# A transformer block on one core: far attention scores from packed copies, softmax statistics on another queue, transposes twelve slots behind

## The chip, the core and the metric

The kernel runs on one core of one Trainium2 chip. The metric is the device time of one execution in microseconds, less being better; the time before is the median of three runs. All arithmetic is fp32 in effect: a matmul operand is split into a high and a low part in the fp32r format, and a product is two or three matmuls.

## The reference

One block over 1024 tokens of 1024 channels: a gated causal convolution branch, a dilated window attention with 16 heads of 64, a gated sum of both, then a feed-forward layer with a short convolution. The attention, which the change is about, is this (cut):

```python
DILATION_GROUPS = ((128, 1), (512, 4), (2048, 16))
for window, dilation in DILATION_GROUPS:
    o_g, lse_g = dilated_window_attention(q, k, v, slopes, window, dilation)
    ...
mix = jax.nn.softmax(jnp.stack(lses), axis=0)
o = jnp.einsum('gbsh,gbshd->bshd', mix, jnp.stack(outs))
...
# in dilated_window_attention: a query sees keys that lie a multiple of `dilation` back, up to `window`
scores = scores - slopes[:, None, None] * dist
scores = jnp.where(valid[None, :, None], scores, -jnp.inf)
m = jnp.max(scores, axis=-1, keepdims=True)
p = jnp.exp(scores - m)
```

The three groups together are one softmax in which a key counts once for each group that it is in, so the kernel adds the logarithm of that count to the score, as part of a mask that holds the slope as well.

## The kernel before

The kernel projects q, k, v (with norms) and parks them in DRAM; then comes the attention loop; then the output projections and the feed-forward layer.

**Units of a head.** The 1024 queries are eight tiles of 128, numbered 0 to 7. Half 0 is tiles 0 to 3; each needs keys of tiles up to its own. Half 1 is tiles 4 to 7 and has two parts. Its *near* part takes the keys of tiles 4 to 7 (for tile 4 also tile 3). Its *far* part takes the keys 0 to 511 that are left; they lie more than 128 tokens back, where only every fourth distance counts, so queries 512 to 1023 and keys 0 to 511 fall into four residues modulo 4, and within a residue 128 queries meet 128 keys. `scored` makes each score with two matmuls (line 916 with the high part of the keys, 917 with the low part), each 128x128 for the far part; before the change their operands are views of q, kh, kl with a step of four elements (`fourth_of`).

**Slots.** The loop runs over `slots`: eight a head, one score unit each. `SCORES` gives them: half 0 has (3), (2), (1), (0); half 1 has far, (7), (6), (4, 5). Before, a head begins with half 1 (places 0 to 3) and then does half 0 (places 4 to 7); only the last head has them the other way. What happens in a slot:

- `score`: matmuls into PSUM, and on VectorE (DVE) `least` (line 920), which adds the mask, takes the maximum and copies to SBUF as tile `pf` (far) or `p`;
- `fill`: steps of a filler, the gate and convolution output products, three matmuls of 128x512 each (names `gate`, `ya`). `FRONT` and `BEHIND` say how many at which of eight places; `START` adds some to the first slots, `TAIL` holds for the slots after the last score. There are 192 steps;
- `flip`: BACK slots after the scores, TensorE transposes the powers into `pp` or `pp_far` (line 1007); ScalarE and DVE split them into `ph`, `pl` (`split`);
- `weigh`: one slot later, the products with v (lines 1044, 1045, output `o`); `result`: ScalarE copies to `ot`, two DMAs write it (`do`);
- `powers`: exp on ScalarE, with the sums, in tile `own` for half 1.

**Normalizing before the transposes.** Half 0's powers are divided by their sums one slot later: `share`, a reciprocal on DVE and a scaling on GpSimd (`times`, line 962). Half 1's queries have two parts in two layouts (near: 128 consecutive tokens on the partitions; far: one residue), so each part needs the other's maximum and sum in its own layout. `give` writes `own` to DRAM (`dst`, 4 KB, the far layout right after the far powers, the near layout after unit (4, 5)); `take` reads `dst` in the other layout into `other`; `combine` makes the factors `both` on DVE and ScalarE, and eight `times` scale the powers on GpSimd, the far ones first. Before, `give` is issued on ScalarE's queue (line 978) and `take` on SyncE's (line 982), and `combine` stands six slots after the far scores.

**Queues.** In this stretch ScalarE, DVE and TensorE keep the written order. SyncE, which issues all loads and most stores and is called the load queue here, and GpSimd are ordered by the build's scheduler. Each engine works its instructions in order: a `take` that waits for its `give` to land holds up what stands behind it on the load queue. `head(h + 1)` loads q, kh, kl (two halves of the partitions each) and the mask m at place 1, `values(h)` loads v (tokens) and vf (residues) at place 0. The tiles q, kh, kl, m, v, vf, own, other, p and pf are double.

Of the kernel before, what the change touches and what calls it, by code (L numbers as in the profile page):

```python
# [14 lines left out]
F32R = mybir.dt.float32r  # L15
# [6 lines left out]
P = 128  # L22
# [3 lines left out]
H = 16  # L26
# [6 lines left out]

LAG = 2
WARM = 7
FRONT = (1, 1, 1, 0, 0, 0, 1, 1)
BEHIND = (1, 0, 1, 1, 1, 0, 1, 0)
BACK = 8
START = (2, 1, 1, 1, 0, 0, 0, 0)
TAIL = (2, 1)  # L40
PLAIN = (10, 11)
LATE = (12, 13, 14, 15)
PAIRS = ((0, 1), (2, 3), (4, 5), (6, 7), (8, 9))
# [15 lines left out]
def block_kernel(ctx: ExitStack, tc: tile.TileContext, x, xT, x0, g2, pack, mask,  # L59
                 w_first, w_ch, w_qkv, w_co, w_ao, w_o, w_up, w_down, out):  # L60
    nc = tc.nc
    act, dve, pool, pe, sp = nc.scalar, nc.vector, nc.gpsimd, nc.tensor, nc.sync
# [7 lines left out]
    def big_ps(name):  # L70
        return psA.tile([P, T], F32, tag="A", name=name)
# [232 lines left out]
    if True:  # L304
# [331 lines left out]
        for ch in range(6):  # L636
            kind, g8 = ch % 3, ch // 3
            wpieces = [wpiece(w_qkv[kind * 2 + g8, :, 2 * j : 2 * j + 2, :], f"qkv{ch}_{j}") for j in range(4)]
            for tt in range(8):
# [3 lines left out]
                if len(tails) > LAG:  # L643
                    t = tails.pop(0)
# [112 lines left out]
        tiles = {}  # L757
# [137 lines left out]
    p2b = p2b_cm.__enter__()  # L895
    if True:
# [4 lines left out]
        def ready2(tag, shape, dt, bufs, name):  # L901
            return laid.pop(tag) if tag in laid else p2b.tile(shape, dt, tag=tag, bufs=bufs, name=name)
# [9 lines left out]
        fourth_of = lambda t, r: t.rearrange("p (j r) -> p r j", r=4)[:, r]  # L912
        by_fourth = lambda t: t.rearrange("p (i a r) -> p i r a", r=4, a=32)

        def scored(s, qs, kh, kl):
            pe.matmul(s, qs, kh, start=True, stop=False)
            pe.matmul(s, qs, kl, start=False, stop=True)  # L917

        def least(pt, s, m, nm):
            dve.tensor_tensor_reduce(out=pt, in0=s, in1=m, scale=-1.0, scalar=3e38,  # L920
                                     op0=ALU.add, op1=ALU.min, accum_out=nm)
# [3 lines left out]
        def score(h, tiles, units):  # L925
            q, kh, kl, m = tiles
            made = []
            if not score_banks:
                pair = big_ps(f"s_{h}_{units[0]}")
                score_banks.extend((pair[:, 512:], pair[:, :512]))  # L930
            s = score_banks.pop()
            tag, size = ("pf", 512) if units == ("far",) else ("p" + "".join(map(str, units)),
                                                            sum((i + 1 - lowest(i)) * P for i in units))
            whole = ready2(tag, [P, size], F32, 2, f"{tag}_{h}")
            if units == ("far",):
                for r in range(4):
                    scored(s[:, r * P : (r + 1) * P], fourth_of(q[:, 512:], r),
                           *(fourth_of(t[:, 0:512], r) for t in (kh, kl)))
                for r in range(4):
                    pt = whole[:, r * P : (r + 1) * P]  # L940
                    pts[h, "far", r] = pt, own[h][:, 1, r]
                    least(pt, s[:, r * P : (r + 1) * P], m[:, 512:640], own[h][:, 1, r, 0:1])
                    made.append(pts[h, "far", r])
                return made
            at = 0
            for i in units:
                ks = slice(lowest(i) * P, (i + 1) * P)
                c = slice(at, at + ks.stop - ks.start)
                at = c.stop
                scored(s[:, c], q[:, i * P : (i + 1) * P], kh[:, ks], kl[:, ks])  # L950
                st = own[h][:, 0, i - 4] if i > 3 else ready2("st", [P, 8], F32, 4, f"st_{h}_{i}")
                pts[h, i] = whole[:, c], st
                made.append((s[:, c], m[:, 512 - c.stop + c.start : 512], *pts[h, i]))
            for sc, mc, pt, st in made:
                least(pt, sc, mc, st[:, 0:1])
            return [u[2:] for u in made]
# [4 lines left out]
        def times(pt, f):  # L961
            pool.tensor_scalar(pt, pt, f, 1.0, op0=ALU.mult, op1=ALU.mult)
# [5 lines left out]
        near_of = lambda t: t.rearrange("(i p) c -> p i c", p=P)  # L968
        far_of = lambda t: t.rearrange("(j r) c -> j r c", r=4)
        own, other = {}, {}  # L970
# [4 lines left out]

        def give(h, layout):
            d = dst_[layout][h]
            act.dma_start((near_of, far_of)[layout](d), own[h][:, layout])

        def take(h, layout):  # L980
            d = dst_[1 - layout][h]
# [2 lines left out]
        def combine(h):  # L984
            o, t = own.pop(h), other.pop(h)
            f = ready2("both", [P, 2, 4], F32, 2, f"both_{h}")
            dve.tensor_tensor(out=f, in0=o[:, :, :, 0], in1=t[:, :, :, 0], op=ALU.subtract)
            dve.tensor_scalar(f, f, 80.0, None, op0=ALU.min)
            act.activation(f, f, AF.Exp)
            dve.tensor_tensor(out=f, in0=f, in1=t[:, :, :, 1], op=ALU.mult)  # L990
            dve.tensor_tensor(out=f, in0=f, in1=o[:, :, :, 1], op=ALU.add)
            dve.reciprocal(f, f)
            for r in range(4):
                times(pts[h, "far", r][0], f[:, 1, r : r + 1])
            for i in (7, 6, 4, 5):
                times(pts[h, i][0], f[:, 0, i - 4 : i - 3])
# [34 lines left out]
        outs, read_out = {}, {}  # L1031
# [27 lines left out]
        def fill(n):  # L1059
            for _ in range(n):  # L1060
                next(gates, None)
# [21 lines left out]
                o_sums.append((raw, hi, lo))  # L1083

        SCORES = (((3,), (2,), (1,), (0,)), (("far",), (7,), (6,), (4, 5)))
        slots = [(h, half, n) for h in range(H) for half in ((1, 0) if h < H - 1 else (0, 1)) for n in range(4)]
        pts = {}
        late, done = [], None
        for tag, n, dt, bufs in (("pf", 512, F32, 2), ("p7", 512, F32, 2), ("p6", 384, F32, 2), ("p45", 512, F32, 2),
# [4 lines left out]
        with tc.manual_schedule(engines={ENG.Activation, ENG.DVE, ENG.PE}):  # L1094
            pend = []
            fill(1)
            for at in range(len(slots) + BACK + 1):
                count[2] += 1
                cur = slots[at] if at < len(slots) else None
                front, behind = (FRONT[at % 8], BEHIND[at % 8] + (START[at] if at < 8 else 0)) if cur else TAIL  # L1100
                new = []
                if cur is not None:
                    h, half, n = cur
                    place = at % 8
                    if place == 0:
                        statistics(h)
                    if place == 0:
                        values(h)
                    if place == 1 and h + 1 < H:
                        tiles[h + 1] = head(h + 1)  # L1110
                    new = score(h, tiles[h], SCORES[half][n])
                for unit in late:
                    share(*unit)
                if len(pieces) > 2:
                    piece_high(2)
                fill(front)
                flips = []
                if BACK <= at < len(slots) + BACK:
                    fh, fhalf, fn = slots[at - BACK]
                    if FLIPS[fhalf][fn]:  # L1120
                        flips.append(flip(fh, fhalf, FLIPS[fhalf][fn]))
                for w in pend:
                    done = weigh(*w) or done
                pend = flips
                late = []
                if done is not None:
                    result(*done)
                    done = None
                if 0 <= at - 6 < len(slots) and slots[at - 6][1:] == (1, 0):
                    combine(slots[at - 6][0])  # L1130
                for unit in new:
                    powers(*unit)
                if cur is not None and half == 0:
                    late = new
                elif cur is not None and n in (0, 3):
                    give(h, 1 if n == 0 else 0)
                    take(h, 0 if n == 0 else 1)
                if at == len(slots):
                    p2_cm.__exit__(None, None, None)
                    hb2.append(ctx.enter_context(tc.tile_pool(name="hb2a", bufs=1, reuse_waits="tile")))  # L1140
                    oT = [[hb2[0].tile([P, KT, 512], F32R, tag=f"hb{a}0", name=f"oT{a}0")] for a in range(2)]
                    heads = [o_fetch(0, k) for k in range(0, KT - 2, 2)]
                if at > len(slots):
                    o_step(heads)
                if at == len(slots) + 4:
                    heads.append(o_fetch(0, KT - 2))
                piece_low()
                fill(behind)
                piece_high(2)
            for _ in gates:  # L1150
                piece_low()
                piece_high()
                o_step(heads)
# [10 lines left out]
    if True:  # L1164
# [210 lines left out]
        with tc.manual_schedule(engines={ENG.Activation, ENG.DVE, ENG.PE}):  # L1375
# [33 lines left out]
            q = cols[0]  # L1409
# [26 lines left out]
            q = cols[1]  # L1436
# [42 lines left out]
    if True:  # L1479
# [49 lines left out]
        for f in range(FT):  # L1529
# [12 lines left out]
            r = ready.pop(0)  # L1542
            with tc.issue_after(settled.ins), tc.issue_after(formed.ins):
# [6 lines left out]
                elif 2 < f + 1 < FT:  # L1550
                    v, w = up_weights(f + 1)
# [6 lines left out]
    with tc.tile_pool(name="ph5", bufs=1, reuse_waits="tile") as p5_:  # L1558
# [142 lines left out]
        for n in range(3):  # L1701
            r = residual(0, n, 1)
# [75 lines left out]
```

## Time and profile before

| | |
|---|---|
| median of three runs | 1793.5 us (1787.94 to 1797.32) |
| the profiled execution | 1794.75 us, its span 1793.0 us |
| mean granted TensorE clock | 0.984 |
| TensorE busy | 1755.0 us |
| the attention loop | about 596.5 to 966 us of the span |

Times in the rows count from the span's start. A row of the groups gives line, engine, operation, tiles written and read, shape and count, then busy us and the mean ns of one, then the engine's idle time before it and what ended that. The clock column is the share of the full TensorE clock that was granted. The DMA share is the mean busy share of the core's 16 DMA engines; it is summed by the packets' starts and can be a little over 1.

### The profile page before, as it was taken

The numbers are of one execution on the slowest core, as the hardware profiler recorded it, in microseconds if no ns is written. First come the engines' busy times: TensorE is split into PE (matmuls) and PEld (weight loads), VectorE is DVE, ScalarE is ACT, GpSimd is POOL, SyncE is SP. The second block draws the span as 40 slices with busy tenths as digits, with TensorE's granted clock in tenths as the row PEclk, the third lists the DMA queues.
The fourth block names the chain that finished last, engine by engine and source line by source line (L and its number), as shares of the span: only waits on it lengthen the run. The fifth ranks groups of instructions, "written<-read, shape, count | busy, mean of one in ns | idle before, by whom it ended". The sixth has DMA issues, their size and how long they took to land.

```text
span 1793.0 us, 22578 instructions
## 1 busy us (share of the span) xinstructions
PE 1755.0 (98%) x8003; PEld 1434.8 (80%) x8003; DVE 1290.6 (72%) x2098; ACT 786.3 (44%) x1351; POOL 176.6 (10%) x252
## 2 busy tenths in 40 slices
PE   9999999999999999899999999999999999999999
PEld 7888888888888777787787788888888888888887
DVE  5999999999866355554545754587777677789863
ACT  5421233223335466565553633454454454543431
POOL 0000231131000122222221000000000000000000
PEclk9999999999999999899999999999999999999999
DMA  9311145245538988977757867542222222389851
GB/s 375 134 45 48 50 129 173 103 136 164 199 113 242 272 174 191 224 190 174 181 132 242 305 218 274 188 153 80 85 83 82 83 76 89 115 321 340 288 180 47
DMA packets 189937, 300.32 MB, mean 168 GB/s; under 512 B 35072, under 2 KB 93056, under 8 KB 189312
## 3 DMA queue, kind: packets, MB, share of 16 engines
q1 hardware_dynamic: 176624, 292.32, 51.7%
q10 hardware_dynamic: 13200, 6.56, 1.3%
q8 instruction: 63, 1.03, 0.2%
q14 instruction: 50, 0.41, 0.1%
HBM read 214.80 MB, written 84.02 MB: 167 GB/s over the span
## 4 chain that ended last, share of the span: by engine, by line
PE 86%; DMA 9%; ACT 2%; DVE 1%; issue 1%; POOL 1%; SPq 1%; ACTq 0%; DVEq 0%; POOLq 0%
PE dx L1584 7%; PE xz L141 6%; PE xz L142 6%; PE xz L143 6%; PE dy L1584 5%; PE qkv L134 5%; PE qkv L135 5%; PE qkv L136 5%; DMA dst<-own 4%; PE y L141 2%; PE y L142 2%; PE y L143 2%; PE wo L135 2%; PE wo L136 2%; PE wo L134 2%; DMA other<-dst 1%
## 5 line engine op out<-in xcount | busy, mean ns | idle before, releaser
L134 PE MATMUL qkv<-hi_qkv,hT 128*128 128x512 f32 x384 | 153.1, 400 | 0.0
L135 PE MATMUL qkv<-lo_qkv,hT 128*128 128x512 f32 x384 | 151.8, 396 | 0.0
L136 PE MATMUL qkv<-hi_qkv,hT 128*128 128x512 f32 x384 | 151.7, 396 | 0.0
L86 DVE TENSOR_TENSOR pl<-pp,ph 128x512 fp32r<-128x512 f32 (+1 forms) x96 | 59.9, 624 | 80.5 <-ACT ph L85 80.0
L1487 DVE SCALAR_TENSOR_TENSOR u<-u,pk 128x1023 f32<-128x1023 f32 x88 | 112.3, 1278 | 1.2 <-ACT u L1485 0.9
L110 POOL TENSOR_TENSOR rs<-ss,mhalf 128x8 f32<-128x8 f32 x32 | 66.2, 2071 | 303.3 <-DVE ss L109 303.3
L584 DVE SCALAR_TENSOR_TENSOR cacc<-csum,both,cacc 128x512 f32<-128x512 f32 x120 | 89.6, 747 | 0.3
L584 DVE SCALAR_TENSOR_TENSOR cacc<-apad,pk,cacc 128x512 f32<-128x512 f32 x120 | 88.6, 747 | 0.0
L136 PEld LDWEIGHTS qkv<-hi_qkv,hT 128*128 128x128 f32 x384 | 72.0, 188 | 17.1
L135 PEld LDWEIGHTS qkv<-lo_qkv,hT 128*128 128x128 f32 x384 | 72.1, 188 | 16.3
L134 PEld LDWEIGHTS qkv<-hi_qkv,hT 128*128 128x128 f32 x384 | 72.0, 188 | 16.4
L584 DVE SCALAR_TENSOR_TENSOR codd<-apad,pk,codd 128x513 f32<-128x513 f32 x112 | 83.9, 750 | 0.7 <-ACT codd L577 0.7
L86 DVE TENSOR_TENSOR lo_uv<-raw_uv,hi_uv 128x1024 fp32r<-128x1024 f32 x20 | 24.5, 1225 | 82.4 <-ACT hi_uv L85 82.4
L85 ACT ACTIVATE ph<-pp 128x512 fp32r<-128x512 f32 (+1 forms) x96 | 52.0, 542 | 54.8 <-PE pp L1007 35.6
L142 PE MATMUL xz<-blk_t,hi_s3g 128*128 128x512 f32 x176 | 69.3, 394 | 0.0
L141 PE MATMUL xz<-blk_t,hi_s3g 128*128 128x512 f32 x176 | 69.3, 394 | 0.0
L143 PE MATMUL xz<-blk_t,lo_s3g 128*128 128x512 f32 x176 | 69.0, 392 | 0.0
L141 PE MATMUL xz<-h2left,hi_uv 128*128 128x512 f32 x176 | 68.9, 391 | 0.0
L143 PE MATMUL xz<-h2left,lo_uv 128*128 128x512 f32 x176 | 68.7, 390 | 0.0
L142 PE MATMUL xz<-h2left,hi_uv 128*128 128x512 f32 x176 | 68.5, 389 | 0.0
L1485 ACT ACTIVATE u<-u,pk 128x1024 f32<-128x1024 f32 x44 | 54.5, 1239 | 9.2 <-DVE u L1474 4.5
L920 DVE CUSTOM_DVE_ANT_0 p<-s,m 128x256 f32<-128x256 f32 (+3 forms) x105 | 49.0, 477 | 12.1 <-PE s L917 12.1
(479 smaller groups left out, 5134.1 us busy)
## 6 DMA issues: line engine op xcount, KB each, us to landing
wr<-w_down SPq DMA_DIRECT2D x45, 512.0 KB, 5.7
gr<-dff SPq DMA_DIRECT2D x62, 256.0 KB, 5.1
raw_qkv<-w_qkv SPq DMA_DIRECT2D x24, 512.0 KB, 5.3
dff<-u SPq DMA_DIRECT2D x22, 512.0 KB, 2.6
raw_uv<-w_up SPq DMA_DIRECT2D x21, 512.0 KB, 3.2
raw_ug<-w_up SPq DMA_DIRECT2D x20, 512.0 KB, 3.2
dv<-v SPq DMA_DIRECT2D x16, 512.0 KB, 2.9
q<-dq SPq DMA_DIRECT2D x32, 256.0 KB, 6.6
```

What stands on the lines that cost most here:

```text
L86: dve.tensor_tensor(out=lo, in0=src, in1=hi.bitcast(F32), op=ALU.subtract)
L110: pool.tensor_tensor(out=dst, in0=tmp, in1=mhalf[:, : tmp.shape[1]], op=ALU.pow)
L134: pe.matmul(ps, ah, hi[:, k % 2, :], start=(k == 0), stop=False)
L135: pe.matmul(ps, ah, lo[:, k % 2, :], start=False, stop=False)
L136: pe.matmul(ps, al, hi[:, k % 2, :], start=False, stop=(k == KT - 1))
L141: pe.matmul(o, wh[:, k, :], bh[:, k, :], start=(start and k == 0), stop=False, skip_group_check=not start)
L142: pe.matmul(o, wh[:, k, :], bl[:, k, :], start=False, stop=False, skip_group_check=not start)
L143: end = pe.matmul(o, wl[:, k, :], bh[:, k, :], start=False, stop=(k == 3), skip_group_check=not start)
L584: dve.scalar_tensor_tensor(out=out_, in0=src[:, i : i + size], scalar=w(i), in1=out_, op0=ALU.mult, op1=ALU.add)
L1485: act.activation(acc, src, AF.Identity, bias=pk[:, C_FB + ci : C_FB + ci + 1], scale=w(2))
L1487: dve.scalar_tensor_tensor(out=acc[:, d:], in0=src[:, : T - d], scalar=w(2 - d), in1=acc[:, d:], op0=ALU.mult, op1=ALU.add)
L1584: pe.matmul(banks[n][:, cols], a[:, c], b[:, d], start=(start and i == 0 and m == 0), stop=(stop and i == nf - 1 and m == 2), skip_group_c ...
```

## The change

Five things are changed, all in the attention loop.

1. A tile `fars` of 3 x 512 columns is added. `by_residue(h)` copies q (queries 512 to 1023), kh and kl (keys 0 to 511) into it with the four residues one after another: three GpSimd copies (line 921). It stands at place 6 of head h - 1 (for head 0 at slot 1). The far scores read `fars`.
2. `give` is issued on the load queue.
3. All heads do half 0 first, then half 1: far scores are at place 4, the near pass follows place 7. `statistics` and `values` go to places 4 and 5.
4. `BACK` is 12, and `combine` stands ten slots after the far scores, two ahead of the far transposes as before. There are four more slots at the end (141 in place of 137).
5. Fillers are placed anew: ten per eight slots as before, but seven ahead of the transposes and three at the slot's end, in place of five and five.

```diff
-FRONT = (1, 1, 1, 0, 0, 0, 1, 1)
-BEHIND = (1, 0, 1, 1, 1, 0, 1, 0)
-BACK = 8
-START = (2, 1, 1, 1, 0, 0, 0, 0)
-TAIL = (2, 1)
+FRONT = (1, 1, 1, 1, 0, 1, 1, 1)
+BEHIND = (1, 0, 0, 0, 1, 0, 1, 0)
+BACK = 12
+START = (1, 1, 1, 1, 0, 0, 0, 0, 0, 0, 0, 0)
+TAIL = (1, 1)
...
+        fars = p2b.tile([P, 3, 512], F32R, name="fars")
+
+        def by_residue(h):
+            views = [t.rearrange("p (j r) -> p r j", r=4) for t in (tiles[h][0][:, 512:], *(t[:, 0:512] for t in tiles[h][1:3]))]
+            outs = [fars[:, n].rearrange("p (r j) -> p r j", r=4) for n in range(3)]
+            for o, v in zip(outs, views):
+                pool.tensor_copy(o, v)
...
-                    scored(s[:, r * P : (r + 1) * P], fourth_of(q[:, 512:], r),
-                           *(fourth_of(t[:, 0:512], r) for t in (kh, kl)))
+                    scored(s[:, r * P : (r + 1) * P], *(fars[:, n, r * P : (r + 1) * P] for n in range(3)))
...
-            act.dma_start((near_of, far_of)[layout](d), own[h][:, layout])
+            sp.dma_start((near_of, far_of)[layout](d), own[h][:, layout])
...
-        slots = [(h, half, n) for h in range(H) for half in ((1, 0) if h < H - 1 else (0, 1)) for n in range(4)]
+        slots = [(h, half, n) for h in range(H) for half in range(2) for n in range(4)]
...
-                front, behind = (FRONT[at % 8], BEHIND[at % 8] + (START[at] if at < 8 else 0)) if cur else TAIL
+                front, behind = (FRONT[at % 8], BEHIND[at % 8] + (START[at] if at < BACK else 0)) if cur else TAIL
...
-                    if place == 0:
+                    if place == 4:
                         statistics(h)
-                    if place == 0:
+                    if place == 5:
                         values(h)
...
+                if cur is not None and place == 6 and h + 1 < H or at == 1:
+                    by_residue(h + 1 if at > 1 else 0)
...
-                if 0 <= at - 6 < len(slots) and slots[at - 6][1:] == (1, 0):
-                    combine(slots[at - 6][0])
+                since = at - BACK + 2
+                if 0 <= since < len(slots) and slots[since][1:] == (1, 0):
+                    combine(slots[since][0])
```

On the load queue, around head 6's statistics, before: `dst_6_107` is its far layout, `dst_6_91` its near one, `other_6186` the tile that the two fetches fill; kh, q, kl and m are of head 8, v and vf of head 7, `do` the results.

```order
L982 DMA other_6186<-dst_6_107 128x4x2
L90 DMA raw_a_6750<-da 128x2x512
L247 DMA dya_137<-ya_0_6320 128x512
L982 DMA other_6186<-dst_6_91 128x8
L1057 DMA do_145<-ot_1_6344 64x512
L1057 DMA do_146<-ot_1_6344 64x512
L152 DMA kh_6488<-dk_0_81 64x1024
L152 DMA q_6487<-dq_0_77 64x1024
L152 DMA v_6444<-dv_83 128x8x128
```

The same place now, first around the far pass:

```order
L152 DMA v_6293<-dv_83 128x8x128
L1064 DMA do_145<-ot_1_6279 64x512
L1064 DMA do_146<-ot_1_6279 64x512
L90 DMA raw_a_6716<-da 128x2x512
L985 DMA dst_6_107<-own_6246 128x8
L247 DMA dya_137<-ya_0_6304 128x512
L989 DMA other_6247<-dst_6_107 128x4x2
L152 DMA kh_6414<-dk_0_81 64x1024
```

and, right behind those, around the near pass:

```order
L152 DMA q_6413<-dq_0_77 64x1024
L152 DMA kl_6415<-dk_1_82 64x1024
L1064 DMA do_145<-ot_0_6380 64x512
L1064 DMA do_146<-ot_0_6380 64x512
L985 DMA dst_6_91<-own_6246 128x4x2
L152 DMA q_6413<-dq_1_78 64x1024
L152 DMA kh_6414<-dk_0_81 64x1024
L989 DMA other_6247<-dst_6_91 128x8
```

The two passes (line 985) have come into this queue, each ahead of its fetch (line 989): one issue stands between the far pass and its fetch, two or three between the near ones; v, two results and a piece of the filler's input stand ahead of the far pass.

On GpSimd, from one head's far scalings to the next one's, before (`both`: half 1's factors, `st`: half 0's):

```order
L962 TENSOR_SCALAR pf_5933<-pf_5933,both_6140 128x128 x4
L962 TENSOR_SCALAR p_5_5987<-p_5_5987,both_6140 128x512
L962 TENSOR_SCALAR p_5_6014<-p_5_6014,both_6140 128x384
L962 TENSOR_SCALAR p_5_6038<-p_5_6038,both_6140 128x256 x2
L962 TENSOR_SCALAR p_5_6117<-p_5_6117,st_1_6120 128x256
L962 TENSOR_SCALAR p_5_6166<-p_5_6166,st_0_6169 128x128
L962 TENSOR_SCALAR p_6_6324<-p_6_6324,st_3_6327 128x512
L962 TENSOR_SCALAR p_6_6359<-p_6_6359,st_2_6362 128x384
```

and now (`kh_6156`, `q_6155`, `kl_6157`: the next head's loads):

```order
L969 TENSOR_SCALAR pf_5732<-pf_5732,both_6082 128x128 x4
L969 TENSOR_SCALAR p_4_5782<-p_4_5782,both_6082 128x512
L969 TENSOR_SCALAR p_4_5804<-p_4_5804,both_6082 128x384
L969 TENSOR_SCALAR p_4_5845<-p_4_5845,both_6082 128x256 x2
L969 TENSOR_SCALAR p_6_6134<-p_6_6134,st_3_6137 128x512
L969 TENSOR_SCALAR p_6_6166<-p_6_6166,st_2_6169 128x384
L969 TENSOR_SCALAR p_6_6199<-p_6_6199,st_1_6202 128x256
L921 COPY fars<-kh_6156 128x512
L921 COPY fars<-q_6155 128x512
L921 COPY fars<-kl_6157 128x512
L969 TENSOR_SCALAR p_6_6222<-p_6_6222,st_0_6225 128x128
L969 TENSOR_SCALAR pf_5992<-pf_5992,both_6347 128x128 x4
```

The three copies stand between three of half 0's scalings and the fourth, and so ahead of the far scalings.

More of the change, by code (lines that the diff above doesn't have):

```diff
@@ L1144, in block_kernel @@
                     o_step(heads)
-                if at == len(slots) + 4:
+                if at == len(slots) + BACK - 4:
                     heads.append(o_fetch(0, KT - 2))
```

## The prediction

> **What bounds the kernel now.** I read the page first, then the busy times by stretch, the waits inside the attention stretch, one far group on the timeline, and the load queue. On the page TensorE is busy nearly always:
>
> ```profile
> span 1793.0 us, 22578 instructions
> PE 1755.0 (98%) x8003; PEld 1434.8 (80%) x8003; DVE 1290.6 (72%) x2098; ACT 786.3 (44%) x1351; POOL 176.6 (10%) x252
> ```
>
> So the 38 us in which TensorE stands still, and matmuls that take longer than they need, are all there is to win. Cut into three stretches, before, in and after the attention loop (core 0: length, busy time of each engine with its instructions, granted TensorE clock, DMA share, GB/s):
>
> ```profile
> 0.00:596.50 596.50, 595.47 (x2633) 481.68 (x2634) 502.36 (x748) 204.97 (x288) 72.26 (x52) 1.00 0.45 153
> 596.50:966.00 369.50, 337.31 (x1745) 279.48 (x1744) 192.58 (x684) 213.12 (x611) 99.10 (x192) 0.93 0.79 186
> 966.00:1793.00 827.00, 822.25 (x3629) 673.69 (x3627) 595.62 (x666) 368.25 (x453) 5.26 (x8) 1.00 0.48 170
> ```
>
> The attention loop has 32 of the 38 idle us, and it alone has a clock under 1.00. No other engine there is near its limit (DVE 193 of 369.5, ACT 213, POOL 99), but the DMA share is 0.79. The waits of that stretch (who, for whom: us, times, longest):
>
> ```profile
> PE pp_far L1007 <- POOL pf L962: 20.0, 15, 2.7
> PE pp_far L1007 <- POOL pf_first L962: 3.5, 1, 3.5
> DVE both L987 <- DMA other<-dst: 44.8, 16, 5.0
> SPq L982 <- DMA dst<-own: 118.2, 32, 6.8
> ```
>
> The far transposes wait for GpSimd's scaling (23.5 us in 16 waits). GpSimd waits for the factors, the factors (DVE) for the fetched statistics, and the fetch on the load queue for the pass to land. That chain ends last in every head. One head on TensorE's timeline (start, length, what):
>
> ```profile
> 743.79 0.43 PE L916 MATMUL s_far<-kh,q 128*128 128x128 f32 x1
> ...
> 745.67 0.43 PE L117 MATMUL ya<-aT,hi_co 128*128 128x512 f32 x1
> ...
> 746.16 0.40 PE L119 MATMUL ya<-aT,lo_co 128*128 128x512 f32 x1
> 749.28 0.47 PE L1007 MATMUL pp_far<-ident,pf 128*128 128x128 f32 x1 [2.72 <-POOL pf L962]
> ...
> 751.97 0.63 PE L119 MATMUL ya<-aT,lo_co 128*128 128x512 f32 x1
> 752.40 0.63 PE L916 MATMUL s_far<-kh,q 128*128 128x512 f32 x1
> ...
> 754.65 0.30 PE L1044 MATMUL o<-ph_far,vf 128*128 128x128 f32 x1
> ...
> 755.58 0.39 PE L916 MATMUL s<-kh,q 128*128 128x384 f32 x1
> ```
>
> Two things are to be seen. Eight strided far score matmuls take 745.67 - 743.79 = 1.88 us, and eight of the same size with packed operands (the far outputs) 755.58 - 754.65 = 0.93. And after the wait the next matmuls take 0.43 from start to start (751.97 to 752.40), where nothing is slower in the program: that is the half clock.
>
> **The change part by part.** *Packed far scores:* 1.88 becomes about 0.93, so 0.95 a head, on TensorE itself, 16 heads: **-15**. Bounds: 0 (if the pace is not the stride's) and -15.
>
> *Twelve slots instead of eight, near half first:* the factors now come ten slots after the far scores and seven after the last near pass is issued; before it was six and three. At 2.68 us a slot (127 slots lie between the first and the last pass, next fence: 340.5 us) three slots were 8.0 us, for a pass that lands after 6.6 and a fetch after 3.1 (below). Seven are 18.8. If the statistics are in time, the 23.5 us of waiting go. With them goes the half clock: 0.07 of 369.5 us is 26 us of lost clock, so 52 us at half. If all 23.5 idle us lie inside it, 14 us of work are lost, if none, 26; the clock falls some time into a wait, so I take **-19**, and with the idle time **-42.5**.
>
> By the Trainium skill (TensorE: Matmul & The Clock Gate, "HAM oscillation — how this bites in real kernels") only gaps of over about 3.4 us bring the half clock, and the longest of these waits is 3.5; by the page the 19 would be missing from the sum. The trace does not agree: half clock follows the wait of 2.72, and 0.93 is the stage's mean.
>
> TensorE's own floor in the stage is then 369.5 - 15 - 42.5 = **312**. More slots add no work: the fillers stay 192 steps, and the tail's slots, 13 for 9, hold two of them instead of three.
>
> *The passes move from ACT's queue to the load queue.* This is what is late next. What the load queue does (start, length of issue; landing of the passes; issues with KB and median us to landing):
>
> ```profile
> 766.99 0.32 SPq L982 DMA_DIRECT2D other<-dst  x1
> ...
> 773.18 0.59 SPq L152 DMA_DIRECT2D kl<-dk  x1
> L978 ACTq DMA_DIRECT2D dst<-own x32: 326/358/438, 599.4 to 939.9; - x32
> DMA to landing us min/median/max: 1.5/6.6/9.8
> raw_co<-w_co SPq DMA_DIRECT2D x8, 512.0 KB, 5.9
> raw_a<-da SPq DMA_DIRECT2D x7, 512.0 KB, 6.9
> dgate<-gs SPq DMA_DIRECT2D x8, 256.0 KB, 5.4
> dya<-ya SPq DMA_DIRECT2D x8, 256.0 KB, 5.9
> kh<-dk SPq DMA_DIRECT2D x28, 256.0 KB, 6.4
> do<-ot SPq DMA_DIRECT2D x60, 128.0 KB, 3.7
> other<-dst SPq DMA_DIRECT2D x32, 4.0 KB, 3.1
> 782.00:784.00 2.00, 2.00 (x15) 1.79 (x14) 1.14 (x4) 1.91 (x4) 0.00 (x0) 1.00 1.11 381
> 784.00:786.00 2.00, 1.98 (x13) 1.50 (x11) 1.76 (x6) 2.00 (x7) 0.69 (x1) 1.00 0.28 35
> 786.00:788.00 2.00, 2.00 (x10) 1.58 (x11) 1.35 (x5) 0.27 (x1) 0.59 (x1) 1.00 0.08 5
> ```
>
> Eleven issues fill 766.99 to 773.77, so 0.62 us each when the queue runs. A head issues six loads of q and k, a mask, v, vf, four results and two fetches (15), 31/16 = 1.9 pieces of the filler, and now two passes: 18.9, or 11.7 us. Behind each pass stands its fetch, which can be issued only when the pass has landed; all later loads and results wait behind that (in the last three rows the DMA engines run dry meanwhile). By the order one issue lies between the far pass and its fetch (0.6 us) and two or three between the near ones (I take three, 1.9). A loop of the queue therefore lasts 11.7 + (Lf - 0.6) + (Ln - 1.9) = 9.2 + Lf + Ln, with Lf and Ln the landing times of the two passes on a queue where the trace never had them. Bounds for each: 1.5 (quiet engines, the last far pass) and 9.8. The far pass is issued while the queue otherwise only waits, so I take the middle of least and median, 4.0; the near one goes out among loads, so the median, 6.6. That is **19.8 a head**, against 312/16 = 19.5 for TensorE averaged with the ends, and less for TensorE in the middle, where no tail is in it. So the queue is late next.
>
> The stage by that: four slots ahead of the first far pass (596.5 to 599.4 now, 2.9 us, and four slots at 312/137 = 2.3: 12 us), 123 slots = 15.4 loops x 19.8 = 305, and 13 tail slots. Nine took 966.0 - 939.9 = 26.1 now, 2.5 each without a last wait like the first one (3.5); less one filler of 0.7, 1.8 each, 24. Together **341**, 28.5 less than 369.5.
>
> *The copies on GpSimd:* three a head, 512 columns each, read with a step of four. Rows of its scalings (mean ns):
>
> ```profile
> L962 POOL TENSOR_SCALAR p<-p,st 128x512 f32<-128x512 f32 x15 | 10.4, 693 | 150.3 <-DVE st L965 119.1 <-PE s L917 31.2
> L962 POOL TENSOR_SCALAR pf<-pf,both 128x128 f32<-128x128 f32 x60 | 26.7, 462 | 79.0 <-DVE both L992 79.0
> L962 POOL TENSOR_SCALAR p<-p,st 128x128 f32<-128x128 f32 x15 | 5.5, 368 | 3.2 <-DVE st L965 3.2
> ```
>
> Between 0.69 each (packed) and 1.39 (twice that, as the stride cost TensorE): 2.1 to 4.2 a head, on an engine that is idle 270 of 369.5 us. I take the middle, 1.04, and count nothing, since they are needed six slots after they are asked for; the price if that cover is gone is a rival below. By the Trainium skill (GPSIMD Engine Reference, "Performance pitfalls for Q7 kernels") a read whose step is over 8 bytes takes about 2.9 cycles an element and not 1.9; as an estimate from that, 0.69 x 2.9/1.9 = 1.05 us. No run here shows it yet.
>
> *Edits at nothing:* v is loaded at another slot, still eight slots ahead of its use; the passes' issues (0.36 us each) leave ACT, which is not late.
>
> **Sum.** The profiled execution took 1794.75 us, 1.25 above the median of the runs. 1794.75 - 28.5 - 1.25 = **1765**.
>
> **The rivals.** *A, the forecast:* the load queue's loop sets the pace, 1765; with Lf + Ln between 9.3 and 11.9 it is 1745 to 1785.
>
> *B, every wait goes:* passes land soon enough (12 + 15.4 loops + 24 is 312 at a loop of 17.9, Lf + Ln of 8.7) and TensorE keeps its floor of 312: 1794.75 - 57.5 - 1.25 = 1736. For it: a pass lands in 1.5 when the engines are quiet, and the seven slots leave room. Against it: the DMA share is 0.79 already.
>
> *C, the copies hold up the scaling:* by GpSimd's order they stand ahead of the far scalings of the head before. From the factors' slot to the transposes' are two slots, 5.0 us; copies at 4.2, one near scaling 0.37 and four far ones 4 x 0.46 = 1.85 make 6.4, so 1.4 late, 16 times: 22, and half clock in the old proportion (19/23.5), 18. 312 + 40 = 352 gives 1776. For it: they also wait for loads; against: only if they start as late as the factors.
>
> *D, slower:* the passes land no sooner behind the loads than they did beside them, 6.6 and 6.6. The loop is 22.4, the stage 12 + 345 + 24 = 381, the time 1805. The point from which it decides is the loop of 21.7 us, Lf + Ln = 12.5. Place: the load queue at the two fetches; TensorE would again wait at the far transposes or for q and k. For it: loads on that queue land after 5.4 to 6.9. Against: while the queue waits for a landing it issues nothing, so the pass has little behind which to stand. The worst of it: three loads, a filler result and two results (1.3 MB) go out just ahead of the near pass; at the 186/0.79 = 235 GB/s of full engines they take 5.6 us, 3.7 of which are gone by its issue (six at 0.62). With 1.9 more for each pass the time is 1805 + 15.4 x 3.8 = 1864. The Trainium skill (DMA: Bandwidth & Descriptors, "Queues, rings and completion order") states the rule behind this rival: each DMA engine takes turns between queues packet by packet, so a small transfer on a queue of its own need not stand behind bulk. The trace agrees little: on its own queue the pass still took 6.6, against 1.5 on quiet engines.
>
> *E, it does not do what it says:* the packed scores keep the old pace (1.88), for instance since the weight loads set it. If the queue sets the pace nothing changes; in B it is 1751.
>
> **How the numbers follow.** A 0.37, B 0.25, C 0.10, E 0.06, D 0.16, and 0.06 for a loop that stops just short of today's (about 1789). A measurement of this kernel tells 0.5%, 9 us, from no change. Faster than 1784.5: nearly all of A (0.34), B, E and most of C (0.09): **0.74**; within: the rest of A and C and the last case, **0.10**; slower: D, **0.16**. Leaving out D and the worst of the last case, the range is **1730 to 1790**.
>
> **What would show it.** Right: far score matmuls at 0.12 from start to start; no wait of pp_far on GpSimd; clock 1.00 in the stage; the load queue's fetches still waiting for the pass some 100 us or more; a stage of about 340 us. Wrong: passes landing later than 6.6, a wait of DVE on the fetch or of TensorE on q, kh, kl, or far scores waiting for fars.

## The result, and the profile after

| | median | runs |
|---|---|---|
| before | 1791.96 us | 20, 1782.39 to 1797.32 |
| after | 1790.49 us | 20, 1786.98 to 1800.05 |

The ratio is 1.000 with a 95% interval of 0.9986 to 1.0014: no change, where 1765 was forecast. The profiled execution of the changed kernel (head of its page):

```profile
span 1789.2 us, 22776 instructions
PE 1744.3 (97%) x8003; PEld 1422.1 (79%) x8003; DVE 1300.4 (73%) x2098; ACT 789.1 (44%) x1351; POOL 223.7 (13%) x300
```

TensorE is busy for 10.7 us less than before (1755.0) and stands still 7 us longer (44.9 of the span; before 38.0). The attention stretch in the same window as before (columns as there):

```profile
596.50:966.00 369.50, 328.94 (x1756) 268.89 (x1755) 203.80 (x685) 216.48 (x613) 142.80 (x237) 0.92 0.73 186
```

The granted clock did not rise (0.93 before, 0.92 now), and the DMA share fell from 0.79 to 0.73 at the same 186 GB/s. The groups of TensorE by shape, before:

```profile
L917 PE MATMUL s_far<-kl,q 128*128 128x128 f32 x60 | 24.9, 415 | 0.0
L916 PE MATMUL s_far<-kh,q 128*128 128x128 f32 x60 | 24.9, 415 | 0.0
```

and after:

```profile
L925 PE MATMUL s_far<-fars 128*128 128x128 f32 x64 | 15.1, 275 | 0.0
L924 PE MATMUL s_far<-fars 128*128 128x128 f32 x64 | 14.3, 261 | 0.0
```

So the packed scores do what was expected: the eight of a head take 0.84 us up to the next instruction (719.35 to 720.19 on the timeline), where 0.93 was taken and 1.88 measured before. The waits of the stretch (who, for whom: us, times, longest), after:

```profile
POOL fars L921 <- DMA kh<-dk: 58.8, 9, 10.8
DVE both L994 <- DMA other<-dst: 27.7, 10, 4.7
PE pp_far L1014 <- POOL pf L969: 17.0, 11, 2.9
PE s L925 <- DMA kl<-dk: 8.3, 6, 3.6
PE s L924 <- DMA kh<-dk: 3.5, 2, 2.2
```

TensorE's wait for the far scaling is still there (17.0 for 23.5), and a new one has come beside it: the scores wait for the loads of k (11.8). Both end at something that the load queue issues. That queue's own waits over the whole span, and the landing of its 32 passes:

```profile
SPq L989 <- DMA dst<-own: 137.6, 32, 6.3
DMA to landing us min/median/max: 2.8/5.9/8.9
```

One loop of the queue on the timeline (start, length of issue; the two fetches are L989, the two passes L985):

```profile
704.71 0.33 SPq L989 DMA_DIRECT2D other<-dst  x1
705.10 0.47 SPq L152 DMA_DIRECT2D kl<-dk  x1
...
708.60 1.48 SPq L1064 DMA_DIRECT2D do<-ot  x2
710.17 0.54 SPq L985 DMA_DIRECT2D dst<-own  x1
710.81 0.49 SPq L90 DMA_DIRECT2D raw_a<-da  x1
716.18 0.37 SPq L989 DMA_DIRECT2D other<-dst  x1
716.65 0.47 SPq L152 DMA_DIRECT2D kh<-dk  x1
...
720.32 0.54 SPq L985 DMA_DIRECT2D dst<-own  x1
...
722.17 0.60 SPq L152 DMA_DIRECT2D kl<-dk  x1
728.04 0.34 SPq L989 DMA_DIRECT2D other<-dst  x1
```

The queue issues from 704.71 to 711.30, waits until 716.18 for the far pass, issues until 722.77, and waits until 728.04 for the near pass: 23.3 us, of which 10.2 are the two landings, and nothing else is between. The chain of waits in the window from 700 to 730 us shows one of the two, by its lines:

```profile
by line: DMA dst<-own 55.2%; DMA kl<-dk 14.1%; DMA other<-dst 11.4%; PE ya L117 5.0%; PE pp_far L1014 4.6%; PE ya L118 4.5%; PE ya L119 4.5%; PE pp L1014 4.0%; PE s L925 4.0%; PE o L1052 2.2%; PE o L1051 2.1%; ACT ph L85 2.0%; PE s L924 1.5
```

The view counts whole pieces, so its shares pass 100%. The passes in it are two near ones, 8.87 us from 695.78 and 7.70 from 720.32; 12.4 of these 16.6 us lie in the window, 41% of it. The far pass is not on this chain: while it lands, the chain goes from kl over TensorE and ScalarE (709.4 to 720.2) and meets the queue again at the near pass, just as the queue's own issues end (720.23). The far passes give the mean loop: the first, the second, the twelfth and the last one, and then the last near one:

```profile
604.10 0.44 SPq L985 DMA_DIRECT2D dst<-own  x1
...
619.44 0.41 SPq L985 DMA_DIRECT2D dst<-own  x1
...
842.64 0.54 SPq L985 DMA_DIRECT2D dst<-own  x1
...
922.17 0.34 SPq L985 DMA_DIRECT2D dst<-own  x1
...
928.52 0.55 SPq L985 DMA_DIRECT2D dst<-own  x1
```

Ten heads from 619.44 to 842.64 are 22.3 us a head. The waits of the queue within these ten heads:

```profile
SPq L989 <- DMA dst<-own: 93.4, 20, 6.3
SPq L985 <- ACT ph L85: 2.8, 5, 1.3
```

That is 9.3 us a head for landings. The other 13.0 are issues, with short waits among them: the view's other rows sum to 26.8 us, 2.7 a head, none longer than 2.4. So the queue is full. Before, in the same window, the loads of the mask (L749) also waited 23.3 us, by the view for loads of v to land:

```profile
SPq L982 <- DMA dst<-own: 73.4, 20, 6.6
SPq L749 <- DMA v<-dv: 23.3, 8, 4.9
```

With the smaller rows, landings other than the passes' held the queue for 37.8 us there, and other engines for 19.7 (0.6 and 26.2 now). So by this view it had no more slack before. Its loop was as long, too: 8 slots of 2.68 are 21.4 us, and 21.1 now if the ends are counted likewise. Whether the queue set the pace already before is not shown: that kernel was not run with its fetches moved.

### The profile page after: what moved, and what is told of

Read it like the earlier page. It is cut to its first block, busy times and chain, and to the rows that moved or that the text cites. A ratio compares the mean times of both kernels' runs of the same rounds, so it can differ in the third digit from the quotient of the medians.

```text
span 1789.2 us, 22776 instructions
## 1 busy us (share of the span) xinstructions
PE 1744.3 (97%) x8003; PEld 1422.1 (79%) x8003; DVE 1300.4 (73%) x2098; ACT 789.1 (44%) x1351; POOL 223.7 (13%) x300
## 4 chain that ended last, share of the span: by engine, by line
PE 88%; DMA 8%; DVE 1%; POOL 1%; ACT 1%; issue 1%; SPq 0%; ACTq 0%; DVEq 0%; POOLq 0%
PE dx L1594 7%; PE xz L141 6%; PE xz L142 6%; PE xz L143 6%; PE dy L1594 5%; PE qkv L134 5%; PE qkv L136 5%; PE qkv L135 5%; DMA dst<-own 4%; PE y L142 2%; PE y L141 2%; PE y L143 2%; PE wo L135 2%; PE wo L134 2%; PE wo L136 2%; PE yb L117 2%
## 5 line engine op out<-in xcount | busy, mean ns | idle before, releaser
L117 PE MATMUL ya<-aT,hi_co 128*128 128x512 f32 x128 | 57.5, 449 | 0.0
```

The costliest lines, as they stand in the source:

```text
L117: pe.matmul(o, hi[:, k, :], ah[:, k, :], start=(k == 0), stop=False)
```

## The experiments

The theories. **Q**: the load queue's loop, its issues and the two landings that it waits out, sets the pace. **M**: the 16 DMA engines are full, and bytes set the pace. **P**: TensorE's own work and its clock set the pace, and the new waits only take up slack. Times are medians, each with its ratio to the kernel before run beside it on the same chip (1792 to 1795).

| kernel | passes / fetches | us | ratio, 95% interval |
|---|---|---|---|
| the change | load queue / at once | 1790.5 | 0.9986 to 1.0014 |
| e1 | ScalarE / at once | 1766.1 | 0.9829 to 0.9895 |
| e12 | far ScalarE, near load queue / at once | 1768.9 | 0.9835 to 0.9882 |
| e13 | near ScalarE, far load queue / at once | 1770.8 | 0.9850 to 0.9891 |
| e2: before, one edit | load queue / at once | 1801.3 | 1.0034 to 1.0074 |
| e3 | load queue / at once, older pass | 1739.8 | 0.9684 to 0.9727 |
| e5 | load queue / on ScalarE | 1789.1 | 0.9953 to 0.9995 |
| e7 | ScalarE / behind other issues | 1752.3 | 0.9748 to 0.9781 |
| e7b | load queue / behind other issues | 1747.9 | 0.9727 to 0.9756 |
| e9: no copies | load queue / at once | 1792.5 | 0.9980 to 1.0011 |
| e8: no copies | ScalarE / at once | 1767.0 | 0.9809 to 0.9861 |
| e11: no copies | load queue / behind other issues | 1755.4 | 0.9756 to 0.9796 |
| e10: before and copies | ScalarE / at once | 1794.3 | 0.9976 to 1.0010 |

**The passes back on ScalarE's queue.** One line of `give`:

```diff
-            sp.dma_start((near_of, far_of)[layout](d), own[h][:, layout])
+            act.dma_start((near_of, far_of)[layout](d), own[h][:, layout])
```

> The changed kernel, with the passes back on ScalarE's queue. Theory Q (the load queue's loop of issues and two waits for landings sets the pace): the loop loses two issues (1.2 us) and part of the two waits, since a pass then leaves as soon as its powers are there and not behind v and the results; at about 18 us a head the stage is some 40 us shorter and the time 1745 to 1765. Rival M (the 16 DMA engines are full, so q, k and the statistics come late whatever the order of the issues): the bytes are the same, the time stays at 1780 to 1795.

1766.1: the move of the passes costs 24 us here. (That this is close to the 1765 forecast is chance: the forecast had the passes on the load queue.) On ScalarE's queue they land no sooner than on the load queue:

```profile
DMA to landing us min/median/max: 2.5/6.0/9.4
```

**The same move alone, on the kernel before** (`act` to `sp` in its `give`, line 978).

> The kernel before, with only the passes moved to the load queue. Q: the loop becomes 9.2 + 5.9 + 6.9 = 22 us, as measured in the changed kernel, and with three slots for the near pass each wait of the far transposes grows: 0.5 to 2.5 us a head, 10 to 40 us in all, 1800 to 1830. M: the same bytes on the same engines, 1785 to 1797.

1801.3, 0.5% slower. There TensorE waits longer at the far transposes (the waits of its profile):

```profile
PE pp_far L1007 <- POOL pf L962: 38.6, 16, 7.5
PE pp_far L1007 <- POOL pf_first L962: 5.1, 1, 5.1
```

43.7 us where it was 23.5. The sign of the move is the same in both kernels, the price is not: 9 us there, 24 in the changed kernel. Why they differ is not settled.

**Only the dependence taken away.** `take` reads the pass of the head before, which landed long ago; the queue has the same issues in the same order, and all bytes. The statistics of two heads are mixed by that: the kernel leaves out the right normalization.

```diff
-            d = dst_[1 - layout][h]
+            d = dst_[1 - layout][max(h - 1, 0)]
```

> The changed kernel, but each fetch reads the statistics that the head before passed (the normalization mixes two heads' statistics; the same number of DMAs, bytes and instructions). No fetch waits for the landing of the pass issued just ahead of it. Q: the loop is 11.7 us of issues, TensorE's floor of about 312 us in the stage is left, 1735 to 1750. M: full DMA engines set the pace: the time stays over 1775.

1739.8. The queue's wait and the stretch in its profile; the stretch is cut where it ends, sooner than before by as much as the span is shorter (966.0 - 55.0):

```profile
SPq L989 <- DMA dst<-own: 24.0, 14, 4.1
```

```profile
596.50:911.00 314.50, 301.88 (x1741) 251.49 (x1740) 197.63 (x680) 213.85 (x608) 144.64 (x237) 0.98 0.90 218
```

With 24.0 us of waiting in place of 137.6 (what the 24.0 are was not traced) the same queue moves 218 GB/s at a share of 0.90 (186 at 0.73 in the changed kernel), and the clock is 0.98. The stretch lasts 314.5 us, close to the floor of 312 that was forecast for TensorE. M falls: the same bytes pass 51 us sooner. The two waits a head hide that much. How much of it the change's other parts bring is not shown, since the kernel before has such waits too (118.2 us) and was not run without them.

**The fetches on ScalarE, three slots after the pass.**

```diff
-            sp.dma_start(other[h][:, layout], (near_of, far_of)[layout](d))
+            act.dma_start(other[h][:, layout], (near_of, far_of)[layout](d))
...
+                    due.append((at + 3, h, 0 if n == 0 else 1))
+                while due and due[0][0] <= at:
+                    take(*due.pop(0)[1:])
```

> The changed kernel, with the fetches on ScalarE's queue, each three slots after its pass (about 6.9 us, a landing takes about 6). The load queue then never waits for a landing, and the result stays that of the reference. Q: as without the wait, 1735 to 1755, a little more than that where ScalarE waits. M: over 1775. If the wait only moves to ScalarE, its groups show an idle time ended by the pass, and the time is 1780 or more.

1789.1: hardly a change. The wait has moved to another in-order engine (waits of its attention stretch, in an execution of 1782.9):

```profile
PE o L1051 <- ACT ph L85: 24.7, 14, 3.9
ACT ph L85 <- DMA dst<-own: 18.9, 5, 4.2
```

ScalarE's copies for the products now stand behind the fetch, and TensorE behind them.

**The fetches behind other issues of their own queue.** The far pass's fetch goes behind the near pass and the results of its slot, the near pass's fetch six slots later behind the next load of vf; nothing else moves. First with the passes on ScalarE (e7), then on the load queue as in the change (e7b):

```diff
-                    take(h, 0 if n == 0 else 1)
+                    if n == 3:
+                        with (tc.issue_after(behind_of["do"].ins) if "do" in behind_of else ExitStack()):
+                            take(h, 0)
+                        due.append((at + 6, h))
...
+                if due and due[0][0] <= at:
+                    with tc.issue_after(behind_of["vf"].ins):
+                        take(due.pop(0)[1], 1)
```

> The changed kernel with the passes on ScalarE's queue and each fetch on the load queue behind work that it does not need: the far one behind the results of the near pass's slot, the near one behind the next head's vf (5 issues, 3 us). Q (the load queue's loop of issues and waits for landings sets the pace): both waits shrink to under 2 us, the loop to some 12 to 15 us, so TensorE's floor is nearly reached: 1738 to 1752. If instead the late fetch makes the factors late, the far transposes wait again and it is over 1766, the time with the passes alone on ScalarE's queue.

> The same, but with the passes on the load queue as in the change. Q: what costs is the wait of a fetch right behind its pass, not the queue on which the pass travels; with the fetches behind other issues it is within 10 us of the one with the passes on ScalarE's queue, 1740 to 1760. If the pass standing behind loads is itself the cost, it stays at 1775 or more.

1752.3 and 1747.9: the second is the best kernel of the study, 2.6% under the one before, with every part of the change kept. Its queue's waits and its stretch (to 966.0 - 47.4):

```profile
SPq L990 <- DMA dst<-own: 26.6, 18, 3.4
```

```profile
596.50:918.60 322.10, 303.70 (x1748) 253.15 (x1747) 193.15 (x682) 214.81 (x611) 144.93 (x237) 0.98 0.90 213
```

The passes land no sooner there, and the fetches later (passes first, then fetches):

```profile
DMA to landing us min/median/max: 2.6/6.0/10.5
DMA to landing us min/median/max: 1.9/5.7/8.6
```

The passes' median is 6.0 for the change's 5.9, the fetches' 5.7 for 2.0. The landings are only, for the most part, no longer waited for. And with the fetches behind, it hardly matters whose queue issues the pass: 4 us, and the two intervals touch.

**The change without the copies** (strided far scores again, no `fars`), with passes on the load queue (e9), on ScalarE (e8), and with the fetches behind (e11).

```diff
-                    scored(s[:, r * P : (r + 1) * P], *(fars[:, n, r * P : (r + 1) * P] for n in range(3)))
+                    scored(s[:, r * P : (r + 1) * P], fourth_of(q[:, 512:], r),
+                           *(fourth_of(t[:, 0:512], r) for t in (kh, kl)))
```

> The changed kernel without the copies: far scores from the strided views, all else as changed. Q: TensorE is not the bound, so the 0.95 us a head come back out of its waits: 1786 to 1797, no change. Rival P (TensorE's own work counts, whatever waits): 15 us slower, 1803 to 1808.

> The changed kernel without the copies and with the passes on ScalarE's queue, so only the twelve slots, the order of the halves and the fillers are left. With the copies it measured 1766. Q: that version is still paced mostly by waits for landings (108 us of them on the load queue), so the copies are worth 0 to 8 there: 1766 to 1774. P: 15 us, 1781.

> The change with its fetches behind other issues of the load queue (e7b, 1748), and without the copies: the far scores read q, kh and kl in steps of four again. Theory Q says that the queue no longer sets the pace there and TensorE does, so the 15 us that the copies take from TensorE must show in the time now: 1758 to 1766. If the queue still set it, or if the copies were worth nothing on any path: 1745 to 1751.

1792.5, 1767.0 and 1755.4, beside 1790.5, 1766.1 and 1747.9 with the copies: nothing, nothing, and 0.0034 of 1793 or 6 us with some 4 of uncertainty. e11's own expectation of 1758 to 1766 missed by 3 us. The heads of the two pages, e11:

```profile
span 1756.7 us, 22662 instructions
PE 1733.7 (99%) x8003; PEld 1422.5 (81%) x8003; DVE 1290.8 (73%) x2098; ACT 788.8 (45%) x1351; POOL 172.3 (10%) x252
```

and e7b:

```profile
span 1745.6 us, 22774 instructions
PE 1720.5 (99%) x8003; PEld 1408.4 (81%) x8003; DVE 1292.3 (74%) x2098; ACT 788.0 (45%) x1351; POOL 225.8 (13%) x300
```

TensorE has 13.2 us more to do in e11, and in these two executions the span is 11.1 longer; by the medians of all runs it is 6 to 7.5. So half of the saving or more shows, and e7b, in which TensorE still stands still for 25.1 us, is not bound by TensorE alone.

Where the saving goes while the queue is full is seen in e9's stretch:

```profile
596.50:966.00 369.50, 329.43 (x1757) 275.96 (x1756) 194.19 (x685) 216.17 (x612) 94.08 (x192) 0.95 0.73 185
```

TensorE is busy 329.4 us there and 328.9 in the change, with the copies. The packed scores need some 13 us less, and TensorE stands still as long (40.1 and 40.6 us), but the clock is 0.92 with them and 0.95 without: 0.03 of 369.5 is 11 us of work. So the time saved comes back as half clock. The clocks of the runs point the same way: 0.981 to 0.986 of the whole execution with the copies, 0.986 to 0.990 without. Why the clock is lower with them was not traced. P falls by e7b: the same program for TensorE takes 43 us less once two fetches stand elsewhere.

**The copies alone on the kernel before.**

> The kernel before with the copies alone: GpSimd lays q, kh and kl out by residue and the far scores read packed operands; eight slots, the old order and the passes on ScalarE's queue stay. By the waits of the profile before (TensorE waits for the far scaling, which waits for the fetch) theory Q expects that the 15 us come back as longer waits: 1785 to 1795. If TensorE's own work is what counts: 1775 to 1780. If the copies hold up the scalings on GpSimd: 1800 or more.

1794.3, no change. TensorE does 13.9 us less there (1741.1 busy) and stands still 48.3 us of the profiled execution in place of 38.0. It gives the saved time back at the far transposes (its waits):

```profile
PE pp_far L1014 <- POOL pf L969: 24.0, 18, 3.4
PE pp_far L1014 <- POOL pf_first L969: 9.1, 1, 9.1
```

33.1 us of waiting for 23.5; 5.6 of the 9.6 more are in the first head.

**One pass alone on ScalarE.**

```diff
-            sp.dma_start((near_of, far_of)[layout](d), own[h][:, layout])
+            (sp, act)[layout].dma_start((near_of, far_of)[layout](d), own[h][:, layout])
```

(layout 1 is the far pass; e13 has the two engines the other way.)

> The change, with the far pass alone issued on ScalarE's queue; the near pass stays on the load queue. Theory Q: the queue's loop loses the far pass's issue and some of the wait for its landing, but keeps the wait for the near one; both passes away were worth 24 us, so one is worth 8 to 16: 1774 to 1783. Were only the near pass at fault, no change (1788 to 1793); were only the far one, all of it (1764 to 1769).

> The change, with the near pass alone issued on ScalarE's queue; the far pass stays on the load queue. Both passes away were worth 24 us (1766), the far one alone 22 to 25 (1769). If the two gains add, the near pass is worth little: 1785 to 1790. If either one frees the queue enough, this too gives about 1769. The load queue's waits for passes should tell: above 130 us in the first case, about 115 in the second.

1768.9 and 1770.8: either one brings nearly all of the 24, so the gains don't add, and e12's expected half was wrong. How the far pass helps is seen on e12's timeline of the pass and its fetch:

```profile
723.13 0.38 ACTq L985 DMA_DIRECT2D dst<-own  x1
...
728.70 0.36 SPq L989 DMA_DIRECT2D other<-dst  x1
```

The pass is under way at 723.13, while the load queue issues v, two results and two more pieces until 727.32; only 1.4 us of the landing are left to wait. In the change these issues came first and the pass behind them. The queue's waits in e12 and e13:

```profile
SPq L989 <- DMA dst<-own: 114.8, 31, 7.1
```

```profile
SPq L989 <- DMA dst<-own: 82.9, 22, 5.8
```

They are 23 and 55 us under the change's, for the same 20 to 22 us of time; the 115 expected of e13 missed. What holds these kernels and e1 near 1766 to 1771 while e7 reaches 1752 is not settled: fetches that still wait are part of it, since moving them took 14 us off e1.

## Why the prediction was wrong, by its own steps

**What is late next** was named rightly: the load queue, whose loop is its issues and two landings. What failed is the size of that loop: 19.8 us a head were taken, 22.3 measured. Of the 2.5, 1.2 are the landing terms: 9.3 a head of waiting in place of (4.0 - 0.6) + (6.6 - 1.9) = 8.1. The other 1.3 are issues: 13.0 in place of 11.7, since these ten heads have 196 of them in the trace, 19.6 a head and not 18.9, at 0.66 and not 0.62 each. The 0.66 holds the short waits for other engines, for which the sum has no term.

The same sum for the kernel before would have warned. Its 16.9 issues a head at 0.62 are 10.5, its waits for passes 118.2/16 = 7.4, together 17.9, where its loop took 21.4: landings of other loads and other engines held the queue for the rest.

The weakest term was **Lf = 4.0**, taken because "the far pass is issued while the queue otherwise only waits". Over the ten heads the far passes landed after 5.9 in the mean, and in six of them nothing stands between the pass and its fetch, where 0.6 was taken. The near ones landed after 6.6, as taken, so the miss in the landing terms is the far pass's.

The queue does not only wait there: the far pass is issued last of a burst. In the loop shown, kl (256 KB), the mask (320), vf (256), two pieces of filler input (512 each), v (512) and two results (128 each) go out in the 5.1 us before it. That is 2.69 MB; at the prediction's 235 GB/s 11.4 us of traffic, 6.3 of it still to come at 710.17, and the pass landed 6.0 after its issue. The two agree in this loop; that the traffic ahead is the cause is argued and not shown. The prediction had done this very sum for the near pass, as "the worst of it" under D, and not for the far one. The near pass of this loop is not explained by such a sum: 1.31 MB lie between the fetch and it, 1.9 us would be left, and it landed after 7.70. What it stood behind is open.

**The sum** had two more misses, of opposite sign. From 596.5 to the first far pass 7.6 us passed where 12 were taken. Behind the last near pass 24 were taken; if the stretch ends as much sooner as the span is shorter (966.0 - 3.8 = 962.2), there were 33.7. In e7b it is much the same (the last near pass at 883.9, the end by the same reckoning at 966.0 - 47.4 = 918.6), so this is not the queue. The likely reason is that the tail's slots hold four more units of transposes and products, which I had counted as if slots were all alike. In sum: -4.4 for the start, 15.4 x (21.07 - 19.8) = +19.5 for the loops (their mean with both ends in it is (928.5 - 604.1) / 15.4), +9.7 for the tail, 24.8, and 341 becomes 366. With the loop as it was taken and the measured ends the forecast would have been 1770.

**The rivals.** The likely one was D's mechanism at its own threshold: it said that from a loop of 21.7 us on nothing would be won, and the loop with its ends is 21.1. Its landings of 6.6 + 6.6 were near (5.9 and 6.6 in the mean of the ten heads), and so were its places: DVE waits for the fetch (27.7), TensorE for k (11.8). Its time of 1805 was not. The reason held against D, that the waiting queue has issued little, is the step that failed; with it D's 0.16 and the last case's 0.06 were held too low. B's price was about right once the landings are out of the way: 1736 forecast, 1739.8 in e3. C falls: where the fetches are at once, the times with and without the copies agree within their intervals (the change and e9, e1 and e8), and where they are moved the copies gain.

**Packed far scores** were right as a term (15 us forecast; TensorE's busy time differs by 13.2 between e11 and e7b), and worth nothing on the path while the queue is full (e9). The Trainium skill (SBUF — State Buffer, "Door 1: The DMA port swizzle") states that a line of SBUF has 16 bytes and that full bandwidth takes at least two accesses to a line. A step of four fp32 makes one access a line, and 1.88 against 0.84 us for eight matmuls agree with that. The copies pack both operands at once, so no run shows which of the two set the pace.

**The copies** were taken at 1.04 us and took 1.10 (median of 16 for each tile). The estimate of 1.05 worked out from the Trainium skill (GPSIMD Engine Reference, "Performance pitfalls for Q7 kernels") agrees with that within 5%.

**The waits of pp_far and the half clock** stayed, as they had to with the factors late; where the queue was freed the clock was 0.98 (e3, e7b). In the changed kernel 0.92 of 369.5 us means 59 us at half clock. The prediction had set aside the rule of the Trainium skill (TensorE: Matmul & The Clock Gate, "HAM oscillation — how this bites in real kernels") that idle gaps of over 3.4 us bring it. The trace agrees with setting it aside: only one of TensorE's waits in this stretch is that long (3.6 us).

**Taking turns between queues.** The Trainium skill (DMA: Bandwidth & Descriptors, "Queues, rings and completion order") states that each DMA engine takes turns between the queues packet by packet. By that one would expect a small pass to land sooner on ScalarE's queue. The runs show no such gain: 6.0 us in the median in e1, 6.6 before, 5.9 on the load queue. What the other queue gives is an earlier issue.

## What to carry to other kernels

A transfer that must wait for another one's landing should not stand right behind it on an in-order queue: leave independent issues between, up to as many as a landing is long (here some 6 us, or ten issues at 0.62, as an estimate). Here that took the queue's wait from 137.6 to 26.6 us without moving anything to another engine. When a step moves into a queue, add up what that queue does in a loop, issues and waits, with the place at which each transfer is issued, and see first whether the same sum gives the loop of the kernel at hand; a margin of 10% on such a sum is no margin. A saving on the busiest engine was worth nothing here until the loop that paces it was shorter than its own work.

## What was not expected of the hardware

A pass of 4 KB took 5.9 to 6.6 us to land in the medians shown, whichever queue issued it, against 1.5 to 2.8 for the quickest. The fetches, 4 KB as well, landed after 2.0 us in the changed kernel, where they go out behind a wait of some 5 us, and after 5.7 in e7b, where they go out among loads. So the time of the same small fetch goes with the traffic around it. And moving two small fetches a head within one queue changed how much of the bandwidth is used at all: 186 GB/s with 137.6 us of waiting behind passes, 213 with 26.6.
